# Mixer A's output projection: column blocks 2 and 3 as a pair with two seven-product units

## The chip, the cores and the metric

The kernel runs on one core of one Trainium2 chip. A core has five engines with a queue of instructions each: TensorE (matmuls; PE, with its weight loads shown as PEld), VectorE (DVE), ScalarE (ACT), GpSimd (POOL) and SyncE (SP, which here issues the weight loads). An engine starts its instructions in the order of its queue; semaphores make one engine wait for another. The metric is the device time of one launch in microseconds (us).

## The reference

The computation is an encoder of two layers on 256 tokens of width 2048, in float32. Layer 0 uses mixer A, layer 1 mixer B, and each is followed by a gated feed-forward block:

```python
for i in range(DEPTH):                       # DEPTH = 2
    hn = rms_norm(h, mix_norm[i])
    h = h + (mixer_a(hn, ...) if i % 2 == 0 else mixer_b(hn, ...))
    h = h + conv_ffn(rms_norm(h, ffn_norm[i]), w_up[i], conv_w[i], conv_b[i], w_down[i])
return rms_norm(h, final_norm)
```

Mixer A is attention with 16 query heads of width 128 and 4 key/value heads, with normalised and rotated queries and keys. Its last step is `o @ w_o`, with `o` of 256 x 2048 and `w_o` of 2048 x 2048. Mixer B ends in the same kind of product with a 3072 x 2048 matrix. The feed-forward block is `(silu(gate) * value) @ w_down` behind a product with `w_up` (2048 x 11264) and a width-3 convolution.

## The kernel before

**A product.** A float32 operand is split into a high part, rounded to the type `fp32r`, and a low part, the rest. A product is made of three matmuls: high x high, high x low, low x high (`feed`, lines 127 to 129). For weights the high part `wh` is written by ACT (L139) and the low part `wl` by DVE (L140). Both have four buffers (`NHL`), as has the raw tile `raw` that SP loads (`NRAW`). One `raw` holds 128 partitions x 1024 columns, two rows of 512.

**Chunks and column blocks.** The 2048 rows of a weight matrix go in chunks of 512 (`kg`, 0 to 3 in mixer A), its columns in blocks of 512 (`n`, 0 to 3). One `feed` multiplies one chunk with one block: two raw tiles, four slices of 128 rows, two halves of the tokens (`m`) and three matmuls, which makes 24 matmuls of 512 columns.

**Mixer A's output projection** is `out_proj`, called without `units`. `project2` does blocks 0 and 1, interleaved by chunk (cut at chunk 2, and chunk 3 last, since its heads leave the attention last). Then `project` does block 2 and, after it, block 3, chunk after chunk. After each block `add_residual` adds the two accumulators to `h` (DVE, L454), `post` takes sums of squares (ACT, L360) and starts `late_transpose`, which turns the block of `h` into the operand `xh` of the feed-forward block: two transposes on DVE (L370), 16 copies shared by POOL and ACT (L391, L389), then four high halves on ACT (L324) and four low halves on DVE (L327). The attention's outputs stand in tiles `a`, split by ACT and DVE (L320, L321).

**Units.** Mixer B's output projection and the feed-forward blocks' down projections have two column blocks done side by side by `pair`, in which a chunk may be a unit: `fast_unit` multiplies it with both blocks in seven products of recombined quarters in place of eight, 7 x 6 = 42 matmuls in place of 48. For that DVE makes four sums of weights (L173) beside seven splits (ACT L174, DVE L175). The products q = 1, 5, 6, 7 stand in the four banks of the pool `ps`, the others add to the accumulators of the two blocks, and `fold` (L187 to L204) brings the four into `h` with eight DVE additions of 512 columns. In mixer B the left operands are recombined by `recombined` (L797 to L817): four additions, eight subtractions on DVE for two chunks, and one split for each chunk.

**What sets the order.** Side work is written as generators. `step()` advances the first in the list `pending`, `step(True)` all in `beside`; each `feed` calls each twice, `fast_unit` four times the one and three times the other. Behind that a scheduler places the instructions of each engine by its own estimate of when they can run; `tc.high_priority` puts splits of weights ahead. What results is a fixed queue on each engine. The feed-forward block begins (`project2` with `late` = 1) with chunks 0, 1 and 2 of its first gate block, then the same of its first value block; chunk k needs block k of the turned `h`.

Of the kernel before, what the change touches and what calls it, by code (L numbers as in the profile page):

```python
# [7 lines left out]
F32 = mybir.dt.float32  # L8
F32R = mybir.dt.float32r
# [4 lines left out]
P = 128  # L14
D = 2048
NT = 256
# [14 lines left out]
def tile_encoder(ctx: ExitStack, tc: tile.TileContext, x, xT, w_a, w_ao, q_gain, k_gain, w_b, w_bo,  # L31
# [25 lines left out]
    def nm(s):  # L57
        uid[0] += 1
        return f"{s}_{uid[0]}"
# [16 lines left out]
        if next(gen, StopIteration) is not StopIteration:  # L76
            pending.append(gen)

    def step(mid=False):
        if mid:  # L80
            beside[:] = [g for g in beside if next(g, StopIteration) is not StopIteration]
            return
        while pending:
            if next(pending[0], StopIteration) is not StopIteration:
                return
            pending.pop(0)
        if spare and next(spare[0], StopIteration) is StopIteration:
            spare.pop(0)

    def drain(keep=0):  # L90
        while len(pending) > keep or beside:
            step(True)
            if len(pending) > keep:
                step()

    extra, count = [None], [0]

    def raw_tile():
        count[0] += 1
        if extra[0] and count[0] % 3 == 0:  # L100
            pool, tags = extra[0]
            tags.append(tags.pop(0))
            return pool.tile([P, 2, 512], F32, tag=tags[0], name=nm("raw"), bufs=2 if len(tags) == 1 else 1)
        return spool.tile([P, 2, 512], F32, tag="raw", name=nm("raw"), bufs=NRAW)

    def of_m(x, m):
# [99 lines left out]
    def pair(wd, ns, lhs, order, spot, folds, post, hurry=0, ready=None):  # L206
# [19 lines left out]
        for i, (kg, side) in enumerate(order):  # L226
            while ready is not None and kg not in ready:
                step()
            if side is None:
                if kg == fasts[0]:  # L230
                    while beside:
                        step(True)
                    while ready is not None and "u" not in ready:
                        step()
                    acc.update({q: ps_tile() for q in (1, 5, 6, 7)})
                later = {s for _, s in order[i + 1:]}
                end = [q for q, s in ((1, None), (5, None), (6, None), (7, None), (2, 0), (4, 0), (3, 1))
                       if not later & {None, s}]
                fast_unit(acc, lhs[-1 - kg], wd[ns[0], kg], wd[ns[1], kg], begun, end, spot)
                if kg == fasts[-1]:  # L240
                    beside.append(closing())
                    if 0 not in later:
                        finish(0)
                continue
            mine = ((2, 4), (3, 8))[side]
            end = not any(s in (side, None) for _, s in order[i + 1:])
            feed(sides[side], lhs, kg, wd[ns[side], kg], not begun.issuperset(mine), end,
                 begun=[m for m in range(2) if mine[m] in begun])
            begun.update(mine)
            for _ in range(hurry):  # L250
                if pending:
                    step()
            if end:
                finish(side)
# [230 lines left out]
    def ffn(l, hT, ss_in, cw, g_next, last, side=None):  # L485
        with tc.tile_pool(name=nm("fpool"), bufs=1) as fp:
# [156 lines left out]
            for hf, (p0, p1) in enumerate(HALVES):  # L643
                slots = {}
# [99 lines left out]

                np_ = p1 - p0
                wd = w_down[l][:, p0:p1]
                extra[0] = fp, ["raw2"]
# [21 lines left out]
    def out_proj(w, slots, kgs, late, g_next, junk, pool, tag, new_quad, cuts=(), units=None):  # L769
# [8 lines left out]
            post(n)  # L778

        if units:  # L780
            fast, own, tmp, spot, folds, raws = units
            done(project2(w, 0, 1, slots, kgs, late, lambda a: done(a, 0), None, cuts,
                          [lambda kg=kg: recombined(kg, slots, own, tmp) for kg in fast]), 1)
            extra[0] = raws
            both = {kg: [(kg, 0), (kg, 1)] for kg in sorted(kgs) if kg not in fast}
            (k0, k1, k2, k3), (f0, f1) = both, fast
            pair(w, (2, 3), slots, both[k0] + both[k1] + [(f0, None)] + both[k2] + [(f1, None)] + both[k3],
                 spot, folds, post)
            extra[0] = None
            drain(1)  # L790
            return hTn, ss
# [58 lines left out]
    def mixer_a():  # L850
        with tc.tile_pool(name="apool", bufs=1) as ap:
# [274 lines left out]
    def mixer_b(hT, ss_in):  # L1126
        with tc.tile_pool(name="bpool", bufs=1) as bp:
# [31 lines left out]
            for hf in range(2):  # L1159
# [160 lines left out]
                for g in range(3):  # L1320
                    accs = project(w_b, 6 * g + 4 + hf, hT, kgs)
                    vs[g] = evac_split(bp, accs, rstd, v12[g - 1] if g else None)
                    if g == 0:
                        start(value_stage())

            def own(kg):
                return pair_tile(bp, [P, 4, NT], "qT" if kg else "kT")

# [10 lines left out]
            return *out_proj(w_bo, slots, [0, 2, 4, 1, 3, 5], 3, 3, junk, bp, "vl", lambda: quad_tile(bp, "stg", 2),  # L1339
                             (), ((0, 2), own, tmp, spot, folds, (bp, ["e0", "e1"]))), cw  # L1340

    hT, ss, cw = mixer_a()
    hT, ss = ffn(0, hT, ss, cw, 2, False, bias_lines)
# [86 lines left out]
```

## Time and profile before

| | us |
|---|---|
| median of 3 runs (2240.21 to 2241.39) | 2241.18 |
| the profiled execution | 2241.6 |
| its span, first to last instruction | 2239.8 |
| mean granted TensorE clock | 0.999 |
| mixer A's block 2 and 3 of the output projection, in the span | about 215.7 to 259.3 |

Times within the span count from its first instruction. In a row of the timeline the first number is the start, the second the duration, and at its end may stand the idle time of the engine just before and what ended it; `x2` at the end merges two instructions that follow each other. A matmul's duration includes what overlaps with the next one, so the distance of two starts is the measure of its cost; the same holds, for a smaller part, on DVE. A row of a tile gives minimum, median and maximum duration in ns, then first and last start. A row of waits gives total us, number and the longest.

### The profile page before, as it was taken

What the parts mean: (1) busy time and instruction counts of PE and PEld (TensorE: products, weight loads), DVE (VectorE), ACT (ScalarE), POOL (GpSimd) and SP (SyncE); (2) the same over time, 40 slices, a digit from 0 to 9 for tenths busy, and PEclk for the clock granted to TensorE, in tenths of its full rate; (3) what the DMA queues carried; (4) which work ended last, traced back from release to release, by engine and by line L of the source; (5) the groups of instructions that cost most, each with busy time, mean ns of one, the idle gap of its engine ahead of it and who ended that gap; (6) DMA issues with size and microseconds to landing.
All of it is one profiled execution on the core that took longest, in us unless ns stands there. A gap on an engine that the chain in (4) does not pass through costs nothing.

```text
span 2239.8 us, 28736 instructions
## 1 busy us (share of the span) xinstructions
PE 2225.2 (99%) x10005; PEld 1843.6 (82%) x10005; DVE 1719.6 (77%) x2211; ACT 1320.1 (59%) x1858; POOL 784.2 (35%) x1035
## 2 busy tenths in 40 slices
PE   9999999999999999999999999999999999999998
PEld 7888888888888888888888888888888888888887
DVE  6877667778876778868876878587777798677795
ACT  7666655666545666755454456566655655455663
POOL 2343255652006563120053006003766500256601
PEclk9999999999999999999999999999999999999999
DMA  8565656555665565665556555556556566555653
GB/s 301 193 217 180 219 187 198 194 192 184 202 213 192 191 194 181 205 199 195 190 187 196 179 189 175 200 185 213 194 184 203 187 207 204 191 196 187 218 198 132
DMA packets 126178, 439.58 MB, mean 196 GB/s; under 512 B 14408, under 2 KB 18248, under 8 KB 126032
## 3 DMA queue, kind: packets, MB, share of 16 engines
q1 hardware_dynamic: 123056, 429.05, 57.2%
q0 software_dynamic: 2688, 8.39, 1.5%
q8 instruction: 78, 1.28, 0.2%
q14 instruction: 68, 0.56, 0.1%
q10 hardware_dynamic: 288, 0.30, 0.0%
HBM read 432.34 MB, written 5.34 MB: 195 GB/s over the span
## 4 chain that ended last, share of the span: by engine, by line
PE 90%; DVE 6%; issue 1%; ACT 1%; POOL 1%; DMA 1%; SPq 0%; DVEq 0%; POOLq 0%; ACTq 0%
PE acc L129 28%; PE acc L128 28%; PE acc L127 28%; DVE wl L175 2%; DVE wl L140 1%; DVE u L173 1%; PE ps L181 1%; PE ps L182 1%; PE ps L180 1%; DMA raw<-in_w_a_dram 1%; PE acc L181 1%; PE acc L182 1%; PE acc L180 1%; DVE cv L542 1%; ACT wh L139 0%
## 5 line engine op out<-in xcount | busy, mean ns | idle before, releaser
L140 DVE TENSOR_TENSOR wl<-raw,wh 128x1024 fp32r<-128x1024 f32 (+1 forms) x748 | 937.4, 1260 | 365.5 <-ACT wh L139 359.2
L139 ACT ACTIVATE wh<-raw 128x1024 fp32r<-128x1024 f32 (+1 forms) x748 | 782.6, 1049 | 643.8 <-PE acc L129 572.5
L127 PE MATMUL acc<-wh,xh 128*128 128x512 f32 x2176 | 849.2, 391 | 0.7 <-ACT wh L139 0.7
L128 PE MATMUL acc<-wl,xh 128*128 128x512 f32 x2176 | 848.2, 390 | 1.3 <-DVE wl L140 1.2
L129 PE MATMUL acc<-wh,xh 128*128 128x512 f32 x2176 | 847.3, 389 | 0.0
L555 POOL COPY u<-quad 32x256 f32<-32x256 f32 x672 | 483.7, 720 | 334.8 <-DVE quad L370 308.5
L128 PEld LDWEIGHTS acc<-wl,xh 128*128 128x128 f32 x2176 | 409.1, 188 | 87.3 <-DVE wl L140 3.8
L127 PEld LDWEIGHTS acc<-wh,xh 128*128 128x128 f32 x2176 | 409.0, 188 | 85.0 <-ACT wh L139 1.4
L129 PEld LDWEIGHTS acc<-wh,xh 128*128 128x128 f32 x2176 | 408.8, 188 | 84.4
L127 PE MATMUL acc<-wh,a 128*128 128x512 f32 x720 | 280.9, 390 | 0.0
L128 PE MATMUL acc<-wl,a 128*128 128x512 f32 x720 | 280.3, 389 | 0.0
L129 PE MATMUL acc<-wh,a 128*128 128x512 f32 x720 | 280.0, 389 | 0.0
L129 PEld LDWEIGHTS acc<-wh,a 128*128 128x128 f32 x720 | 135.1, 188 | 28.3 <-DVE a L321 0.2
L128 PEld LDWEIGHTS acc<-wl,a 128*128 128x128 f32 x720 | 135.2, 188 | 27.7
L127 PEld LDWEIGHTS acc<-wh,a 128*128 128x128 f32 x720 | 135.2, 188 | 27.5
L374 POOL COPY wide<-quad 32x256 f32<-32x256 f32 x133 | 89.1, 670 | 169.3 <-DVE quad L370 159.8
L391 POOL COPY wide<-quad 32x256 f32<-32x256 f32 x88 | 53.3, 605 | 223.4 <-DVE quad L370 155.7
L482 ACT ACTIVATE stg<-acc,rstd 128x512 f32<-128x512 f32 x122 | 82.9, 686 | 33.9 <-PE acc L129 33.9
L572 POOL TENSOR_TENSOR cv<-cg,cv 128x1024 f32<-128x1024 f32 x18 | 58.2, 3232 | 105.5 <-DVE cv L542 100.1
L174 ACT ACTIVATE wh<-raw 128x1024 fp32r<-128x1024 f32 x56 | 59.5, 1062 | 53.7 <-PE acc L129 48.9
L542 DVE SCALAR_TENSOR_TENSOR cg<-u,cw,cg 128x256 f32<-128x256 f32 x176 | 82.3, 511 | 4.5 <-ACT cg L534 4.5
L525 POOL MEMSET u<- 128x4 f32 x12 | 1.0, 106 | 231.3 <-DVE wl L175 211.0
(284 smaller groups left out, 2006.7 us busy)
## 6 DMA issues: line engine op xcount, KB each, us to landing
raw<-in_w_up_dram SPq DMA_DIRECT2D x352, 512.0 KB, 4.6
raw<-in_w_down_dram SPq DMA_DIRECT2D x176, 512.0 KB, 4.5
raw<-in_w_b_dram SPq DMA_DIRECT2D x144, 512.0 KB, 4.3
raw<-in_w_bo_dram SPq DMA_DIRECT2D x48, 512.0 KB, 4.2
raw<-in_w_a_dram SPq DMA_DIRECT2D x40, 512.0 KB, 4.7
raw<-in_w_ao_dram SPq DMA_DIRECT2D x32, 512.0 KB, 4.5
raw<-in_w_a_dram SPq DMA_DIRECT2D x16, 256.0 KB, 5.9
there<-quad POOLq DMA_DIRECT2D x6, 512.0 KB, 3.5
```

What stands on the lines that cost most here:

```text
L127: nc.tensor.matmul(accs[m], xh, wh[:, j, :], start=st, stop=False)
L128: nc.tensor.matmul(accs[m], xh, wl[:, j, :], start=False, stop=False)
L129: nc.tensor.matmul(accs[m], xl, wh[:, j, :], start=False, stop=sp)
L139: nc.scalar.activation(wh[:, c], r[:, c], AF.Copy)
L140: nc.vector.tensor_tensor(wl[:, c], r[:, c], wh[:, c].bitcast(F32), ALU.subtract)
L174: nc.scalar.activation(wh, r, AF.Copy)
L374: nc.gpsimd.tensor_copy(o[32 * c:32 * c + 32, :, 32 * q:32 * q + 32], quad[32 * q:32 * q + 32, c])
L391: nc.gpsimd.tensor_copy(dst, src)
L482: nc.scalar.activation(o[:, m, :], accs[m], AF.Copy, scale=rstd[:, m:m + 1])
L542: nc.vector.scalar_tensor_tensor(cj, halves(flat[:, j, o:o + NT])[:, ::-1], tap(n, j, i), cj, ALU.mult, ALU.add)
L555: nc.gpsimd.tensor_copy(o, src)
L572: made.append(eng.tensor_tensor(cv, cg, cv, ALU.mult).ins)
```

## The change

In mixer A, blocks 2 and 3 now go through `pair`, in the order chunk 2 (block 2, block 3), chunk 0 as a unit, chunk 3 (block 2), chunk 1 as a unit, chunk 3 (block 3). `recombined` for chunks 0 and 1 starts at the end of `project2`. The order of chunks is now given by the caller; mixer B's stays as it was. The recombination's four tiles (`tmp`), and every third raw tile during the pair, take their space from the four buffers of a tag `pT`, which holds the turned probabilities of the attention: high and low part now stand in one tile of `[P, 2, 4, P]` where they had a tile each. `pair` steps the side work until a unit's operands are there, and `step` and `drain` take a number of generators to leave unstarted (`keep`).

```diff
-    def step(mid=False):
+    def step(mid=False, keep=0):
...
             pending.pop(0)
+            if pending and len(pending) <= keep:
+                return
...
             if len(pending) > keep:
-                step()
+                step(keep=keep)
...
-            return pool.tile([P, 2, 512], F32, tag=tags[0], name=nm("raw"), bufs=2 if len(tags) == 1 else 1)
+            return pool.tile([P, 2, 512], F32, tag=tags[0][0], name=nm("raw"), bufs=tags[0][1])
...
             if side is None:
+                while -1 - kg not in lhs:
+                    step()
...
         if units:
-            fast, own, tmp, spot, folds, raws = units
+            fast, order, own, tmp, spot, folds, raws = units
...
-            both = {kg: [(kg, 0), (kg, 1)] for kg in sorted(kgs) if kg not in fast}
-            (k0, k1, k2, k3), (f0, f1) = both, fast
-            pair(w, (2, 3), slots, both[k0] + both[k1] + [(f0, None)] + both[k2] + [(f1, None)] + both[k3],
-                 spot, folds, post)
+            pair(w, (2, 3), slots, order, spot, folds, post)
...
-            rp = ap.tile([P, 2, 2, P], F32, tag="pTh", name="rp", bufs=4)
-            gbs = ap.tile([P, 4, P], F32, tag="pTl", name="gbs", bufs=4)
+            rp = ap.tile([P, 2, 2, P], F32, tag="pT", name="rp", bufs=4)
+            gbs = ap.tile([P, 4, P], F32, tag="pT", name="gbs", bufs=4)
...
             def new_pT():
-                return pair_tile(ap, [P, 4, P], "pT", 4)
+                t = ap.tile([P, 2, 4, P], F32R, tag="pT", name=nm("pT"), bufs=4)
+                return t[:, 0], t[:, 1]
...
+            def own(kg):
+                return pair_tile(ap, [P, 4, NT], "qT" if kg else "kT")
+
+            def tmp():
+                return ap.tile([P, 4, NT], F32, tag="pT", name=nm("tmp"), bufs=4)
+
+            def spot(i):
+                return ap.tile([P, 2, 512], F32, tag=("vh", "vl", "ro")[i], name=nm("sum"))
+
+            def folds():
+                return [ap.tile([P, 2, 512], F32, tag=t, name=nm("fold")) for t in ("stg", "ro")]
+
+            order = [(2, 0), (2, 1), (0, None), (3, 0), (1, None), (3, 1)]
             return *out_proj(w_ao, slots, kgs, 1, 1, junk, ap, "t2",
-                             lambda: pair_slot(16, [P, 4, 8, 32], name="quad"), (2,)), cw
+                             lambda: pair_slot(16, [P, 4, 8, 32], name="quad"), (2,),
+                             ((0, 1), order, own, tmp, spot, folds, (ap, [("pT", 4)]))), cw
```

More of the change, by code (lines that the diff above doesn't have):

```diff
@@ L746, in ffn @@
                 wd = w_down[l][:, p0:p1]
-                extra[0] = fp, ["raw2"]
+                extra[0] = fp, [("raw2", 2)]
                 if last and hf == 1:
@@ L1324, in mixer_b @@
                         start(value_stage())
+            both = {kg: [(kg, 0), (kg, 1)] for kg in (1, 3, 4, 5)}
+            order = both[1] + both[3] + [(0, None)] + both[4] + [(2, None)] + both[5]
             def own(kg):
@@ L1339, in mixer_b @@
             return *out_proj(w_bo, slots, [0, 2, 4, 1, 3, 5], 3, 3, junk, bp, "vl", lambda: quad_tile(bp, "stg", 2),
-                             (), ((0, 2), own, tmp, spot, folds, (bp, ["e0", "e1"]))), cw
+                             (), ((0, 2), order, own, tmp, spot, folds, (bp, [("e0", 1), ("e1", 1)]))), cw
     hT, ss, cw = mixer_a()
```

## The prediction

> **What bounds the kernel now.** I read the totals first, then who waits for whom, then windows, then the order of instructions in time. The totals, and one row of the chain that ended last:
>
> ```profile
> span 2239.8 us, 28736 instructions
> PE 2225.2 (99%) x10005; PEld 1843.6 (82%) x10005; DVE 1719.6 (77%) x2211; ACT 1320.1 (59%) x1858; POOL 784.2 (35%) x1035
> PE 90%; DVE 6%; issue 1%; ACT 1%; POOL 1%; DMA 1%; SPq 0%; DVEq 0%; POOLq 0%; ACTq 0%
> ```
>
> TensorE (PE) is busy for 99% of the span: a matmul that goes is worth its full pitch, a wait costs its full length. All waits of PE:
>
> ```profile
> PE ps L336 <- DVE qTl L321: 2.0, 1, 2.0
> PE ps L181 <- DVE wl L175: 1.6, 4, 0.4
> PE acc L128 <- DVE wl L140: 1.2, 3, 0.6
> PE acc L127 <- ACT wh L139: 0.7, 1, 0.7
> ```
>
> There are few, and all but one are for VectorE (DVE): it is next in line. Four windows (us; busy PE, PEld, DVE, ACT, POOL; granted clock; DMA): mixer A's output projection, the units of mixer B's, the units in a feed-forward block, and a stretch at half clock.
>
> ```profile
> 205.00:259.00 54.00, 54.00 (x239) 44.59 (x239) 36.77 (x46) 39.13 (x69) 13.06 (x24) 1.00 0.58 192
> ...
> 1478.00:1519.00 41.00, 41.00 (x183) 33.95 (x182) 36.35 (x37) 25.69 (x29) 1.13 (x1) 1.00 0.53 181
> 535.00:560.00 25.00, 24.63 (x107) 19.73 (x106) 23.25 (x26) 14.30 (x17) 0.00 (x0) 1.00 0.54 182
> ...
> 145.00:148.40 3.40, 3.40 (x11) 2.82 (x11) 2.12 (x4) 1.08 (x4) 0.00 (x0) 0.51 0.90 278
> ```
>
> Where the change is made, DVE works 36.77 of 54 us and PE never waits. Where units run, DVE works 36.35 of 41 and 23.25 of 25.
>
> **The change part by part.** *Matmuls.* A chunk of two column blocks costs 2 x 24 matmuls plain and 7 x 6 = 42 as a unit, so two units save 12. TensorE's order in time:
>
> ```profile
> 204.82 0.40 PE L127 MATMUL acc<-wh,a 128*128 128x512 f32 x1
> ...
> 207.11 0.62 PE L129 MATMUL acc<-wh,a 128*128 128x512 f32 x2
> ...
> 259.28 0.39 PE L127 MATMUL acc<-wh,xh 128*128 128x512 f32 x1
> ...
> 270.16 0.39 PE L127 MATMUL acc<-wh,xh 128*128 128x512 f32 x1
> ...
> 303.70 0.39 PE L128 MATMUL acc<-wl,xh 128*128 128x512 f32 x1
> ```
>
> From 270.16 to 303.70 lie 148 steps of 0.2266 us, all on the path: 12 x 0.2266 = **-2.7 us**. This is all that the change can win, and 0.12% of the span; about 0.2% (4.5 us) is what a measurement of this kernel can tell from no change.
>
> *DVE's new work.* It is costed by start-to-start times. Mixer B's fold and feed-forward entry, then the recombination's tiles:
>
> ```profile
> 1508.58 2.35 DVE L140 TENSOR_TENSOR wl<-raw,wh 128x1024 fp32r<-128x1024 f32 x2
> 1510.85 0.68 DVE L195 TENSOR_TENSOR fold<-ps,fold 128x512 f32<-128x512 f32 x1
> 1511.45 0.68 DVE L197 TENSOR_TENSOR fold<-ps,fold 128x512 f32<-128x512 f32 x1
> ...
> 1516.41 1.30 DVE L370 STREAM_TRANSPOSE quad<-h 128x512 f32<-128x512 f32 x2
> 1517.64 1.18 DVE L140 TENSOR_TENSOR wl<-raw,wh 128x1024 fp32r<-128x1024 f32 x1
> ```
> ```profile
> 268.29 1.66 DVE L327 SCALAR_TENSOR_TENSOR xh<-wide,gain,xh 128x256 fp32r<-128x256 f32 x4
> ```
> ```profile
> L802 DVE TENSOR_TENSOR tmp<-a x4: 679/723/879, 1384.6 to 1393.0; 128x512 f32<-128x512 f32 x4
> L809 DVE TENSOR_TENSOR tmp<-tmp x4: 409/420/610, 1388.3 to 1430.7; 128x256 f32<-128x256 f32 x4
> L809 DVE TENSOR_TENSOR tmp<-tmp,tmp x4: 418/464/611, 1391.1 to 1432.6; 128x256 f32<-128x256 f32 x4
> ```
>
> So a split or sum of 1024 columns takes 2.27/2 = 1.14, a 512-column add 0.60, a quad transpose 0.62, a low half of xh 0.41. Neighbours overlap by some 0.08, so a recombining add takes 0.64, a subtraction 0.34 or 0.38. A unit has 7 splits and 4 sums: 11 x 1.14 = 12.5 us of DVE under 42 x 0.2266 = 9.5 us of PE. Mixer B lays two plain feeds (10.9 us of PE, four splits, 4.6 of DVE) between its units; here there is one (5.4 against 2.3).
>
> *First wait: the last attention outputs.* In the changed kernel's DVE order most of the recombination of both chunks (4 adds, 4 subtractions) stands ahead of the last split `a` of the attention, which chunk 3 needs. DVE there, before:
>
> ```profile
> 200.77 1.22 DVE L140 TENSOR_TENSOR wl<-raw,wh 128x1024 fp32r<-128x1024 f32 x1
> 201.91 0.42 DVE L321 TENSOR_TENSOR a<-ps,a 128x256 fp32r<-128x256 f32 x1
> 202.24 1.73 DVE L140 TENSOR_TENSOR wl<-raw,wh 128x1024 fp32r<-128x1024 f32 x1
> 203.89 0.74 DVE L321 TENSOR_TENSOR a<-ps,a 128x256 fp32r<-128x256 f32 x2
> 205.40 1.23 DVE L140 TENSOR_TENSOR wl<-raw,wh 128x1024 fp32r<-128x1024 f32 x1 [0.76 <-ACT wh L139]
> 206.54 0.42 DVE L321 TENSOR_TENSOR a<-ps,a 128x256 fp32r<-128x256 f32 x1
> ```
>
> Inserted are 4 x 0.64 + 2 x 0.34 + 2 x 0.38 = 4.0 us, less the 0.76 idle at 205.40: 3.2. The split ends at 206.96 + 3.2 = 210.2. PE wants it at 207.11, and with two matmuls of the other block now ahead (0.45) at 207.6: a wait of **2.6** (1.5 to 3.5). Behind it on PE stand all later matmuls, behind the split on DVE all later weight splits.
>
> *Second wait: feed-forward entry.* DVE's queue from 210.2 to the split of the second weight piece of feed-forward chunk 0: 4 subtractions 1.5; 24 splits 27.4; 8 sums 9.1; splits of the two recombined operands 2.3; 8 residual adds 4.8; 8 fold adds 4.8; 6 quad transposes 3.7; 8 low halves 3.3. Sum **56.9**, ending at 267.1 without one idle moment. The last 11 of these (two residual adds of block 3, six adds of the fold, two transposes of block 2, the split: 7.2 us) cannot start before the projection's last matmuls have ended, and the split that PE wants 3.2 us into the feed-forward block stands behind them all.
>
> DVE will also idle, above all at the low halves of block 1, which follow eight POOL copies begun by a transpose shortly before:
>
> ```profile
> 1517.87 6.04 POOL L391 COPY wide<-quad 32x256 f32<-32x256 f32 x8 [53.42 <-ACT wh L139]
> ```
>
> The copies take 6.0 and ACT's half 0.5, while DVE has about 5.2 to do in between (three splits, three adds): some 1.3 us; starts that wait for matmuls add a little. I take 1.7 (0.5 to 3.5), hence 268.8. PE started that piece 14 matmuls after 259.28, at 262.45: late by **6.3**, which contains the first wait and the 2.7 saved.
>
> *One-hot matmuls.* The changed order runs the four bias-table matmuls inside this wait; here they stand, on PE's path:
>
> ```profile
> 368.24 0.47 PE ps L1121 x2
> 379.62 0.47 PE ps L1121 x2
> ```
>
> Their 4 x 0.2266 = 0.9 us go there: **-0.9**.
>
> *Block 2's turn.* Chunk 2 of the feed-forward block needs the turned block 2, formerly made under block 3. Walked the same way (transpose, 6.0 us of copies, halves, transposes of block 3), its second weight split is late by **0.8** (0 to 2); mixer B's entry has a wait of this kind, within PE's 1.2 above.
>
> *Clock.* Half clock follows one wait of the trace:
>
> ```profile
> 142.45 0.28 PE L335 MATMUL ps<-kTl,qTh 128*128 128x256 f32 x1
> 144.68 0.41 PE L336 MATMUL ps<-kTh,qTl 128*128 128x256 f32 x1 [1.95 <-DVE qTl L321]
> ...
> 145.54 0.63 PE L127 MATMUL acc<-wh,xh 128*128 128x512 f32 x1
> ...
> 148.10 0.51 PE L127 MATMUL acc<-wh,xh 128*128 128x512 f32 x1
> ```
>
> Six steps take 2.56 us there, 0.427 each: 3.4 us at 0.51 lose 3.4 x (1 - 0.2266/0.427) = 1.6. The entry wait (6.3 + 2.7 - 2.6 - 0.9, less about 1 us lost inside the units: some 4.5) is over twice 1.95, so I count it once, less what block 2's lateness hides: **+1.0** (0 to 3, if the first wait does it too).
>
> The Trainium skill ("TensorE: Matmul & The Clock Gate", Part 1) has the half clock come only after an idle window of about 3.4 us. The row above differs: a wait of 1.95 us sufficed. By the page the first wait would be free of it and the clock term 0 to 1.0 (a sum of 6.0 to 7.0 us), by the row up to 1.6 more.
>
> *At nothing.* Shared pT tiles hold the same bytes in the same number, and the order on DVE, ACT and PE up to the recombination is unchanged; a slip there is 0 to 1 us. Weight loads on SP now also wait for the recombination's tiles; they stand a unit (9.5 us) ahead of their use, and a load lands sooner:
>
> ```profile
> raw<-in_w_ao_dram SPq DMA_DIRECT2D x32, 512.0 KB, 4.5
> ```
>
> The `keep` edit moves halves and transposes at mixer B's entry, where a wait of about 0.5 may go or grow: **-0.2** (-0.5 to +0.5).
>
> Sum: 6.3 - 0.9 + 0.8 + 1.0 - 0.2 = **+7.0 us**. The profiled execution took 2241.6 (span 2239.8), 0.4 above the median of 2241.18; on the median, **2248.2**.
>
> **Rivals.** *DVE keeps up* (not slower): the splits stay ahead by wh/wl's four buffers, and only the 12 matmuls show: 2241.2 - 2.7 = 2238.5. For it: mixer B's units ran with PE 41.00 of 41. Against: the tighter spacing and the fold behind the last matmul. It decides if DVE's queue ends below 262.45 - 2.7 = 259.7, that is if 56.9 us shrink by 7.
>
> *The delay is half hidden*: DVE never idles (4.6 late), the clock stays full, block 2 is in time: 4.6 - 0.9 - 0.5 = +3.2, 2244.4.
>
> *Loads become the wait*: loads of w_down stand ahead of w_up's in SP's queue at the feed-forward entry and wait for block 2's halves; if they hold up two w_up loads by 2 us each, and both waits halve the clock, +7.0 + 4 + 1.6: 2253.8.
>
> **How the numbers follow.** Forecast (between +4.5 and +11.3) 0.70; half hidden (-1 to +4.5) 0.17; keeps up 0.09; loads 0.04. The forecast's own range by its bounds is 2245.7 to 2252.5. Half of the half-hidden case brings the low end to 2243.0, which leaves about 0.2 outside. Slower by over 0.2%: 0.70 + 0.04 and a little for median scatter, 0.75; faster needs more than the 2.7 saved, 0.02; within, 0.23.
>
> **What would show it.** 12 fewer matmuls; a wait of PE near 207 for DVE's `a`; one of 4 to 5 us near 264 for `wl`; a clock below 1.00 after it; DVE busy for over 90% from 205 to 270. Wrong if these waits stay under 1 us each, or if PE waits for loads.

## The result and the profile after

| | before | after |
|---|---|---|
| median, us | 2240.49 (6 runs) | 2252.93 (6 runs, 2251.47 to 2256.04) |
| the profiled execution | 2241.6 | 2252.98 |
| its span | 2239.8 | 2251.2 |
| mean granted clock | 0.999 | 0.996 |

The change makes the kernel slower, by a ratio of 1.0058 with a 95% interval of 1.0047 to 1.0068, 12.4 us by the medians. The forecast was 2248.2, with 2252.5 as the upper end of its range: the direction was right, the size too small.

The totals of the profile after:

```profile
span 2251.2 us, 28764 instructions
PE 2226.7 (99%) x9993; PEld 1843.9 (82%) x9993; DVE 1747.3 (78%) x2247; ACT 1328.8 (59%) x1867; POOL 791.3 (35%) x1035
```

The 12 matmuls are gone (x10005 became x9993), and the span is 11.4 us longer. So TensorE loses about 14 us to waits and to a lower clock. Its waits, after, beside two that were there before, 1.5 us at the start of the kernel and 1.9 in the attention (total us, number, longest; lines from 100 on are a few higher than before, L142 and L177 are the splits `wl`, L325 the split `a`):

```profile
PE acc L130 <- DVE wl L142: 5.7, 2, 5.5
PE acc L131 <- DVE a L325: 2.5, 2, 1.7
PE ps L183 <- DVE wl L177: 2.3, 5, 0.8
PE ps L182 <- ACT wh L176: 1.7, 1, 1.7
PE acc L129 <- ACT wh L141: 1.0, 1, 1.0
```

The timeline shows where the new ones stand (start, duration, and idle time of PE before):

```profile
203.82 0.40 PE L130 MATMUL acc<-wl,a 128*128 128x512 f32 x1
205.07 0.50 PE L131 MATMUL acc<-wh,a 128*128 128x512 f32 x1 [0.85 <-DVE a L325]
...
207.26 0.39 PE L130 MATMUL acc<-wl,a 128*128 128x512 f32 x1
209.33 0.73 PE L131 MATMUL acc<-wh,a 128*128 128x512 f32 x2 [1.68 <-DVE a L325]
...
232.36 0.39 PE L184 MATMUL acc<-wh,kTl 128*128 128x512 f32 x1
234.47 0.50 PE L182 MATMUL ps<-wh,kTh 128*128 128x512 f32 x1 [1.72 <-ACT wh L176]
235.72 0.50 PE L183 MATMUL ps<-wl,kTh 128*128 128x512 f32 x1 [0.76 <-DVE wl L177]
...
236.75 0.56 PE L184 MATMUL ps<-wh,kTl 128*128 128x512 f32 x1
...
240.63 0.39 PE L182 MATMUL ps<-wh,kTh 128*128 128x512 f32 x1
...
267.00 0.40 PE L1138 MATMUL ps<-oh,rl 128*24 128x512 f32 x1
272.88 0.80 PE L130 MATMUL acc<-wl,xh 128*128 128x512 f32 x1 [5.48 <-DVE wl L142]
...
278.23 0.39 PE L129 MATMUL acc<-wh,xh 128*128 128x512 f32 x1
```

By distances of starts, less one pitch of 0.2266: the first wait has two pieces, 1.02 and 1.84 us (2.9); the first unit waits 1.88 and 1.03 (2.9); the feed-forward entry waits 5.65. Behind two of these places the clock halves. The windows below (busy time of PE, PEld, DVE, ACT, POOL; then the granted clock) are laid on the borders at which the clock changes, 3.413 us apart:

```profile
206.11:209.52 3.41, 1.73 (x8) 1.13 (x7) 3.38 (x6) 0.00 (x0) 0.00 (x0) 1.00 0.74 265
209.52:212.94 3.42, 3.42 (x16) 2.81 (x16) 2.93 (x7) 2.06 (x3) 0.00 (x0) 1.00 0.64 182
...
233.42:236.83 3.41, 1.61 (x6) 1.12 (x7) 2.38 (x3) 3.41 (x5) 0.00 (x0) 1.00 0.01 5
236.83:240.24 3.41, 3.41 (x10) 2.67 (x9) 3.41 (x4) 1.82 (x3) 0.00 (x0) 0.50 0.00 0
...
267.55:270.96 3.41, 0.00 (x0) 0.00 (x0) 3.41 (x6) 2.23 (x7) 0.00 (x0) 1.00 0.00 0
270.96:274.37 3.41, 1.50 (x4) 1.21 (x5) 3.41 (x5) 3.21 (x9) 2.46 (x2) 0.50 0.10 29
274.37:277.79 3.42, 3.42 (x10) 2.65 (x9) 1.12 (x1) 0.77 (x2) 3.17 (x7) 0.50 0.91 303
```

Three windows at half clock are new. The starts give their price: from 236.75 to 240.63 ten steps take 3.88 us where 2.27 is usual, a loss of 1.6; from 272.88 to 278.23 thirteen steps take 5.35 where 2.95 is usual, a loss of 2.4. The first of the last two windows costs little, since TensorE still waits in most of it.

So: 2.9 + 2.9 + 5.65 + 1.6 + 2.4 - 2.7 (matmuls) = 12.7. The four one-hot matmuls stand in no term: both kernels run them, here ahead of the entry wait, at 266.31 to 267.00. Measured directly, the matmul that starts at 195.00 before starts at 193.78 after, and the first one of the feed-forward block's down projection starts at 521.40 before and at 533.26 after. So the stretch between them became 13.1 us longer; waits too short for the list make the rest. Ahead of it the kernel after is 1.2 us earlier (0.81 of this is a wait at 136.4 in the attention, which comes and goes with the experiments' kernels), and 0.45 us of a wait at 1527.3, in the feed-forward block behind mixer B, is gone: 13.1 - 1.2 - 0.45 gives the 11.4 between the spans.

DVE, over the stretch for which the prediction asked for more than 90%:

```profile
205.00:270.00 65.00, 58.17 (x244) 46.32 (x244) 59.92 (x74) 44.13 (x66) 15.24 (x16) 0.97 0.45 154
```

59.92 of 65 us is 92%.

### The profile page after: what moved, and what is told of

It reads as the page before. It is cut to its first block, busy times and chain, and to the rows that moved or that the text cites. A ratio compares the mean times of both kernels' runs of the same rounds, so it can differ in the third digit from the quotient of the medians.

```text
span 2251.2 us, 28764 instructions
## 1 busy us (share of the span) xinstructions
PE 2226.7 (99%) x9993; PEld 1843.9 (82%) x9993; DVE 1747.3 (78%) x2247; ACT 1328.8 (59%) x1867; POOL 791.3 (35%) x1035
## 3 DMA queue, kind: packets, MB, share of 16 engines
q8 instruction: 78, 1.28, 0.2%
## 4 chain that ended last, share of the span: by engine, by line
PE 83%; DVE 5%; issue 1%; ACT 1%; POOL 0%; POOLq 0%; DVEq 0%; ACTq 0%
PE acc L130 26%; PE acc L131 26%; PE acc L129 26%; DVE wl L177 2%; PE ps L183 1%; PE ps L184 1%; DVE u L175 1%; PE ps L182 1%; PE acc L183 1%; PE acc L184 1%; PE acc L182 1%; DVE wl L142 0%; DVE cv L546 0%; PE ps L1290 0%; PE ps L336 0%
## 5 line engine op out<-in xcount | busy, mean ns | idle before, releaser
L142 DVE TENSOR_TENSOR wl<-raw,wh 128x1024 fp32r<-128x1024 f32 (+1 forms) x740 | 926.5, 1259 | 344.9 <-ACT wh L141 339.0
L141 ACT ACTIVATE wh<-raw 128x1024 fp32r<-128x1024 f32 (+1 forms) x740 | 773.8, 1049 | 632.8 <-PE acc L131 555.5
L131 PE MATMUL acc<-wh,a 128*128 128x512 f32 x688 | 267.6, 389 | 2.5 <-DVE a L325 2.5
L129 PE MATMUL acc<-wh,a 128*128 128x512 f32 x688 | 268.4, 390 | 0.0
L130 PE MATMUL acc<-wl,a 128*128 128x512 f32 x688 | 267.9, 389 | 0.0
L131 PEld LDWEIGHTS acc<-wh,a 128*128 128x128 f32 x688 | 129.1, 188 | 30.2 <-DVE a L325 3.4
L129 PEld LDWEIGHTS acc<-wh,a 128*128 128x128 f32 x688 | 129.2, 188 | 26.4
L130 PEld LDWEIGHTS acc<-wl,a 128*128 128x128 f32 x688 | 129.2, 188 | 26.4 <-DVE wl L142 0.2
L395 POOL COPY wide<-quad 32x256 f32<-32x256 f32 x88 | 62.1, 706 | 249.2 <-DVE quad L374 187.8
L378 POOL COPY wide<-quad 32x256 f32<-32x256 f32 x133 | 88.1, 663 | 168.3 <-DVE quad L374 159.8
L176 ACT ACTIVATE wh<-raw 128x1024 fp32r<-128x1024 f32 x64 | 68.0, 1062 | 56.2 <-PE acc L131 48.8
L177 DVE TENSOR_TENSOR wl<-raw,wh 128x1024 fp32r<-128x1024 f32 x64 | 77.9, 1223 | 2.8 <-ACT wh L176 2.3
```

The costliest lines, as they stand in the source:

```text
L129: nc.tensor.matmul(accs[m], xh, wh[:, j, :], start=st, stop=False)
L130: nc.tensor.matmul(accs[m], xh, wl[:, j, :], start=False, stop=False)
L131: nc.tensor.matmul(accs[m], xl, wh[:, j, :], start=False, stop=sp)
L141: nc.scalar.activation(wh[:, c], r[:, c], AF.Copy)
L142: nc.vector.tensor_tensor(wl[:, c], r[:, c], wh[:, c].bitcast(F32), ALU.subtract)
L176: nc.scalar.activation(wh, r, AF.Copy)
```

## The experiments

All ratios are to the kernel before, measured on the same chip as the kernel in question; their intervals are 0.0009 to 0.0013 to either side (2 to 3 us), so differences of less than that between two experiments are not taken for settled by the ratios. The last table of this part puts them side by side.

**Are the units the cause, or the tiles and the `keep` edit?**

```diff
-                             lambda: pair_slot(16, [P, 4, 8, 32], name="quad"), (2,),
-                             ((0, 1), order, own, tmp, spot, folds, (ap, [("pT", 4)]))), cw
+                             lambda: pair_slot(16, [P, 4, 8, 32], name="quad"), (2,)), cw
```

> The changed kernel without the two units: blocks 2 and 3 of mixer A's output projection go one after the other again (plain feeds), while the shared pT tiles and the keep edit stay. Theory (VectorE's queue around the units makes all of the loss): the time of the kernel before, 2240.5 us, give or take 0.5 (the keep edit alone: PE's wait of 0.4 to 0.5 us at mixer B's entry may go); no wait of PE near 207, 233 or 267 us. Rival (the shared pT tiles or the keep edit cost something of their own): 2242 us or more, with a new wait in the attention or at mixer B's entry.

Measured: 0.9994 (0.9986 to 1.0003). From 195 to 330 us PE has no wait at all. Shared tiles and `keep` cost nothing that can be measured; the units carry the whole loss.

**Is it the sum of VectorE's work?** First its largest part is left out, then also the recombination. In `fast_unit`, for mixer A alone (`bare`):

```diff
-        t1, t2, t4 = (spot(i) for i in range(3))
+        t1, t2, t4 = (b22, b12, b21) if bare else (spot(i) for i in range(3))
...
-                if q in sums:
+                if q in sums and not bare:
                     nc.vector.tensor_tensor(*sums[q], ALU.add)
...
```

> The changed kernel with the eight sums of weights left out in mixer A's two units (the three splits of each unit that take a sum take a raw tile instead, so the output projection is not the reference's); all else stays. It takes 8 x 1.14 = 9.1 us from VectorE alone; TensorE, ScalarE and the loads do the same as before. Theory (VectorE's sum of work decides the entry): the entry wait (6.0 us with what follows) falls under 1 us, both half-clock stretches go (4.8 us lost), the first wait (2.9) stays since it lies ahead of the units: ratio 0.9995 to 1.001. Rival (the chain through the last matmul, fold, transposes and GpSimd decides, or the loads): an entry wait of over 3 us and a half clock behind it stay, ratio 1.003 or more.

Measured: 1.0017 (1.0008 to 1.0027). PE's waits between 195 and 330 us, all of them:

```profile
PE acc L131 <- DVE a L325: 2.7, 2, 1.7
PE acc L130 <- DVE wl L142: 1.3, 2, 1.0
PE acc L183 <- DVE wl L177: 0.3, 1, 0.3
```

The entry wait is 1.0 in place of 5.5, the unit's waits are gone, no half clock is left in that stretch, and the first wait stays, as the theory said; 1.0017 is a little above its range. Taking 9.1 us of DVE's work gave back 9.2 us (1.0058 - 1.0017 of 2240); that the two agree so closely is chance, since each ratio is known to 2 or 3 us. The fold stands in the same place as in the changed kernel, so the chain behind the last matmul alone does not make the long entry wait. One thing else changed with the sums: GpSimd's copies of block 0 took 4.48 us in place of 9.76, those of block 1 took 9.92 in place of 6.07 (see below). Then:

```diff
+    def plain_quarters(kg, slots):
+        (hi0, lo0), (hi1, lo1) = ([slots["t", kt][:, o::2, :] for o in range(2)] for kt in (4 * kg, 4 * kg + 2))
+        left, right = (hi0[:, :, :P], lo0[:, :, :P]), (hi1[:, :, P:], lo1[:, :, P:])
+        slots[-1 - kg] = {q: left if q in (1, 5, 6, 3) else right for q in range(1, 8)}
+        yield
...
-                          [lambda kg=kg: recombined(kg, slots, own, tmp) for kg in fast]), 1)
+                          [lambda kg=kg: plain_quarters(kg, slots) if late == 1 else recombined(kg, slots, own, tmp) for kg in fast]), 1)
```

> The changed kernel with mixer A's eight sums of weights and its whole recombination left out (the units multiply raw tiles and plain quarters of the attention's output, so the output projection is not the reference's); units, order, fold and loads stay. It asks whether the units are worth their 12 matmuls once VectorE's extra work is gone: 9.1 us of sums, 5.5 of recombination and 2.3 of splits less than in the changed kernel. Theory: no first wait, no wait in the units, an entry wait of at most 1 us (the fold is still behind the last matmul), no half clock after it: 2.7 us saved less 0 to 1: ratio 0.9988 to 0.9995. Rival (the pair has a cost beside VectorE's sums and recombination, such as the fold's chain): ratio 1.0005 or more.

Measured: 1.0004 (0.9995 to 1.0013), between the two expectations and nearer to the rival's. The first wait is gone. But the 2.7 us do not show even now; PE's waits from 195 to 330 us are

```profile
PE ps L183 <- DVE wl L177: 0.8, 1, 0.8
PE acc L130 <- DVE wl L142: 0.6, 2, 0.4
PE ps L182 <- ACT wh L176: 0.3, 1, 0.3
```

With the sums and the recombination the pair loses 12 to 13 us; with neither it about breaks even. Why the last 2 to 3 us do not show, beyond these short waits, stays open.

**Where the first wait comes from, and what it is worth.** The recombination's twelve operations go to GpSimd (`eng` is `nc.gpsimd` in mixer A):

```diff
-            nc.vector.tensor_tensor(r[:, 2 * b:2 * b + 2], hi.bitcast(F32), lo.bitcast(F32), ALU.add)
+            eng.tensor_tensor(r[:, 2 * b:2 * b + 2], hi.bitcast(F32), lo.bitcast(F32), ALU.add)
...
-            nc.vector.tensor_tensor(s[:, o], x, y, ALU.subtract)
+            eng.tensor_tensor(s[:, o], x, y, ALU.subtract)
```

> The changed kernel with mixer A's four additions and eight subtractions of the recombination on GpSimd instead of VectorE. Theory (the recombination ahead of the last split a makes the first wait): the gaps at 203.8 and 207.3 us (2.9 us together) shrink under 0.5; VectorE has 5.5 us less to do, 1.5 of it behind the first wait, so the entry wait near 267 us (6.0 with what follows) falls by about 1.5 at most; in all 3 to 4.5 us less, about 2249. GpSimd may be late with the subtractions; then a wait stands at the first unit near 232 us. Rival (the first wait comes from the pT tiles that the recombination and the extra raw tiles share, or from a load): the first wait stays, 2252.9.

Measured: 1.0069 (1.0055 to 1.0082). The first wait fell from 2.5 to 0.8 in the waits (under 0.5 was expected), so the recombination on DVE makes most of it. But the time did not fall, against the expected 2249. A row of DVE and the last of the recombination on POOL:

```profile
226.77 1.23 DVE L175 TENSOR_TENSOR sum<-raw,raw 128x1024 f32<-128x1024 f32 x1 [6.48 <-DMA raw<-in_w_ao_dram]
```
```profile
216.24 2.54 POOL L810 TENSOR_TENSOR tmp<-tmp,tmp 128x256 f32<-128x256 f32 x2
```

GpSimd needs until 218.8 for the recombination. An extra raw tile lies in the space of `tmp`; DVE stood idle for 6.48 us for its load. Without the extra raw tiles:

```diff
-                             ((0, 1), order, own, tmp, spot, folds, (ap, [("pT", 4)]), nc.gpsimd)), cw
+                             ((0, 1), order, own, tmp, spot, folds, None, nc.gpsimd)), cw
```

> The recombination on GpSimd as before, and the extra raw tiles taken out as well. With the recombination on GpSimd alone VectorE idled 6.5 us for a weight load into a tile of the space that the late recombination still used. Theory (that load is why 5.5 us less of VectorE work won nothing): the idle of 6.5 us goes, the first wait stays at about 1 us, the first unit waits under 1.5 us, the entry wait is 2 to 4 us: ratio 1.002 to 1.004. Rival (GpSimd's recombination is too slow in itself, some 21 us from 202 to 223 us, and the first unit waits for its operands, or copies behind it come late): over 3 us of waits near the first unit stay, ratio 1.0055 or more.

Measured: 1.0052 (1.0039 to 1.0066); the idle of 6.48 us is gone, the entry wait is 3.3. The ratio lies between the two expectations; the rival's sign came true, waits of 3.7 us stand in the units. The other way to take the first wait away starts the recombination behind the loop over blocks 0 and 1:

```diff
-            done(project2(w, 0, 1, slots, kgs, late, lambda a: done(a, 0), None, cuts,
-                          [lambda kg=kg: recombined(kg, slots, own, tmp) for kg in fast]), 1)
+            behind = [lambda kg=kg: recombined(kg, slots, own, tmp) for kg in fast]
+            if late == 1:
+                accs = project2(w, 0, 1, slots, kgs, late, lambda a: done(a, 0), None, cuts)
+                for gen in behind:
+                    start(gen())
+                done(accs, 1)
...
```

> The changed kernel with the recombination of both chunks started behind the attention's end instead of at the end of the loop over blocks 0 and 1; of its eight operations ahead of the attention's last split, four remain (two additions, two subtractions, 2.0 us in place of 4.0). Theory (VectorE's sum of work decides, waits only move): the first wait falls from 2.9 to about 1.2 us, and what is gained comes back as a wait in the units or at the entry, since VectorE does the same work until then: ratio 1.005 to 1.006, as the changed kernel. Rival (waits add up one by one): 1.5 to 2 us are gained, ratio 1.0045 to 1.005, with the entry wait as long as before.

Measured: 1.0047 (1.0034 to 1.0059). The first wait is 1.3, the entry waits 4.0 and 1.0 in two places, with one stretch of half clock in place of two. The ratio lies on the edge between the two expectations and does not tell them apart. The profile does, in part: the stretch from 195 to 521 us is 9.9 us longer than before, where it was 13.1, so 3.2 us were gained, more than the rival expected. The waits did not only move: the first unit's went too, and gaps of 1.3 and 0.9 us came up in the second.

**Do the extra raw tiles matter, taken alone?**

```diff
-                             ((0, 1), order, own, tmp, spot, folds, (ap, [("pT", 4)]))), cw
+                             ((0, 1), order, own, tmp, spot, folds, None)), cw
```

> The changed kernel without the extra raw tiles: during the pair every weight load goes into the four usual raw buffers, none into the space of the turned probabilities. Theory (VectorE's queue makes the waits, loads do not): no wait of PE goes, the ratio to the kernel before stays at 1.005 to 1.0065; if anything loads now come later, in the first unit. Rival (the loads into shared tiles, queued behind the recombination that uses them, make the wait near 232 us): the gaps at 232 to 235 us (2.9 together) and the half clock at 236 us (1.6 lost) go, ratio 1.0035 to 1.004.

Measured: 1.0062 (1.0048 to 1.0075). The rival's gaps did go (2.9 became 0.5), and the half clock behind them. Yet the time is the same: at 248 to 251 us stand two new gaps of 0.8, and the entry wait grew from 5.5 to 6.4. Here a wait taken away ahead of a full DVE queue came back further down. So loads are not what bounds this stage. That the gaps went does not by itself make loads their cause: in this kernel block 0's copies also took 5.27 us only, since they ran ahead of DVE's sums (see below), and the run does not separate the two:

```profile
219.16 5.27 POOL L395 COPY wide<-quad 32x256 f32<-32x256 f32 x8 [17.55 <-DVE quad L374]
```

**Is the fold behind the last matmul to blame?**

```diff
-            order = [(2, 0), (2, 1), (0, None), (3, 0), (1, None), (3, 1)]
+            order = [(2, 0), (0, None), (2, 1), (1, None), (3, 0), (3, 1)]
```

> The changed kernel with the pair's order chunk 2 (block 2), unit 0, chunk 2 (block 3), unit 1, chunk 3 (block 2), chunk 3 (block 3): two plain feeds behind the last unit, as mixer B has them, so that the fold of the units need not stand behind the last matmul. Theory A (VectorE's queue is full from 209 to 272 us, so its sum decides): what VectorE does is the same, the entry wait loses at most 1 to 2 us, and waits in the units, which now have one feed less ahead of them, grow by as much: 2251 to 2255 in all. Theory B (the fold behind the last matmul makes the entry wait): the six fold additions and two residual additions, 4.8 us, leave the stretch behind the end, the entry wait falls from 6.0 to under 2 us and the half clock after it goes (3.2 us lost): about 2246.

Measured: 1.0046 (1.0034 to 1.0059), between A and B and nearer to A. Both effects showed: the entry wait fell to 2.1 us with one stretch of half clock, and the units, which had less work ahead of them, have six gaps of 0.4 to 0.8 us, 3.3 by distances of starts. The fold's place is a part of the entry wait, worth less than the 7 us that B promised.

**GpSimd's copies.** In the changed kernel the eight copies of block 0's turn took 9.76 us, where the prediction assumed 6.0. ScalarE's high halves waited for them, and the split `wh` of the unit's first sum stood behind those. POOL's, ACT's and DVE's rows of after:

```profile
221.97 9.76 POOL L395 COPY wide<-quad 32x256 f32<-32x256 f32 x8 [20.23 <-DVE quad L374]
...
231.76 1.71 ACT L328 ACTIVATE xh<-wide,gain 128x256 fp32r<-128x256 f32 x4 [3.27 <-POOL wide L395]
233.37 1.04 ACT L176 ACTIVATE wh<-sum 128x1024 fp32r<-128x1024 f32 x1
...
232.30 0.49 DVE L331 SCALAR_TENSOR_TENSOR xh<-wide,gain,xh 128x256 fp32r<-128x256 f32 x1 [1.28 <-ACT xh L328]
234.44 1.23 DVE L177 TENSOR_TENSOR wl<-sum,wh 128x1024 fp32r<-128x1024 f32 x1 [1.65 <-ACT wh L176]
```

Block 0's copies all on ScalarE:

```diff
-            if i % 2:
+            if i % 2 or act:
...
-            start(late_transpose(hTn, n, g_next, pool, tag, new_quad))
+            start(late_transpose(hTn, n, g_next, pool, tag, new_quad, tag == "t2" and n == 0))
```

> The changed kernel with all 16 copies of block 0's turn on ScalarE (8 of them were on GpSimd, where they took 9.76 us beside VectorE's run of sums and splits). Theory (GpSimd's slow copies hold up ScalarE's high halves and with them the split wh of the first unit's sum, queued behind): PE's gaps at 232.4 and 234.5 us (2.9 together) and the half clock at 236.6 us (1.6 lost) go, and VectorE's 1024-column splits and sums at 223 to 231 us come back from about 1.34 us apart to 1.14; VectorE loses 2.9 us of idle time, so the entry wait grows no more than PE's start of it moves ahead: 2248 to 2250 in all. Rival (the first unit is late because four sums and seven splits are too much for VectorE in one place, whatever GpSimd does): gaps of 2 us or more stay near 232 us, 2252 to 2254.

Measured: 1.0053 (1.004 to 1.0065), above the theory's range, in the rival's, and not clear of the changed kernel's interval. The gaps at the unit fell from 2.9 to 0.9 and the half clock behind them went, so the rival's sign is absent; but a new gap of 1.2 us stands at 256 and the entry wait is as long as ever. From the last split `a` to the split that ends the entry wait DVE needs 61.6 us in place of 63.5, and the stretch from 195 to 521 us is 11.6 us longer than before in place of 13.1: some 1.5 us were gained, where 3 to 5 were expected. DVE idles anew, 0.54 and 1.30 us, for splits `wh` of ScalarE, which now has all the copies. DVE's sums beside the copies came back to their pace, as expected; first a group of after from 222.9 to 231.1, then the same of this kernel from 216 to 233 (last columns: busy us, mean ns, idle):

```profile
L175 DVE TENSOR_TENSOR sum<-sum,raw 128x1024 f32<-128x1024 f32 x2 | 2.8, 1412 | 0.0
```
```profile
L175 DVE TENSOR_TENSOR sum<-sum,raw 128x1024 f32<-128x1024 f32 x2 | 2.4, 1218 | 0.0
```

**One unit.** With half of DVE's extra work, a wait that goes should stay gone. Three steps, each on top of the one before:

```diff
-            order = [(2, 0), (2, 1), (0, None), (3, 0), (1, None), (3, 1)]
+            order = [(1, 0), (1, 1), (2, 0), (0, None), (2, 1), (3, 0), (3, 1)]
...
-                             ((0, 1), order, own, tmp, spot, folds, (ap, [("pT", 4)]))), cw
+                             ((0,), order, own, tmp, spot, folds, (ap, [("pT", 4)]))), cw
```

> The changed kernel with one unit instead of two: chunk 1 plain in both blocks, chunk 2 (block 2), unit 0, then three plain feeds. TensorE saves 6 matmuls (1.36 us). Theory (VectorE's queue): of the 19.4 us that two units add to VectorE (recombination 5.5, splits of the recombined operands 2.3, fold 4.8, sums 9.1, less two splits 2.3) 12.2 remain, against 17 us that it idles in the kernel before between 205 and 259 us; the first wait falls from 2.9 to about 0.7, the entry wait from 6.0 to under 1.5, no half clock follows: ratio 0.9995 to 1.001. Rival (the entry wait is the chain through the fold, the transposes and GpSimd's copies, which one unit has as well): entry wait over 3 us with a half clock, ratio 1.003 or more.

Measured: 1.0021 (1.0012 to 1.0031), between the two. No wait over 0.9 us at the entry and no half clock, but a first wait of 1.8 and waits of 2.1 in the unit. In this order three feeds stand behind the unit, so the run doesn't separate the fold's place from DVE's smaller sum of work.

The second step starts the recombination late, by the edit shown above:

> The kernel with one unit, its recombination also started behind the attention's end (one addition and two subtractions fewer ahead of the last split). With one unit VectorE has room, so here a wait that goes should stay gone: the first wait of 2.2 us falls under 1, ratio 1.001 to 1.002 (1.0021 with the early recombination). If it comes back elsewhere, 1.002 or more.

Measured: 1.0028 (1.0017 to 1.0039): the first wait fell to 0.9, but it came back elsewhere, as 2.8 and 0.5 in the unit. GpSimd's copies stand ahead of it again:

```profile
224.80 10.66 POOL L395 COPY wide<-quad 32x256 f32<-32x256 f32 x8 [4.91 <-DVE xh L331]
```
```profile
235.50 1.70 ACT L328 ACTIVATE xh<-wide,gain 128x256 fp32r<-128x256 f32 x4 [4.71 <-POOL wide L395]
237.11 1.04 ACT L176 ACTIVATE wh<-raw 128x1024 fp32r<-128x1024 f32 x1
```

ACT stood 4.71 us at the head of a queue in which the unit's next split came right behind, and two stretches of half clock followed (237.5 to 244.3). The third step takes the copies of blocks 0 and 1 from GpSimd (`n < 2` in the edit for block 0):

> The kernel with one unit and late recombination, and all copies of the turns of blocks 0 and 1 on ScalarE instead of half of them on GpSimd. With one unit the waits in the unit (2.8 us) stood behind ScalarE's high halves, which waited for GpSimd's copies. If that is their cause, they fall under 1 us and the ratio to the kernel before is 0.9998 to 1.001, the 1.36 us of saved matmuls against what is left of the waits; if ScalarE (6.7 us of copies in each turn) becomes late itself, the waits stay and the ratio is 1.0015 or more.

Measured: 1.0016 (1.0007 to 1.0024). The two waits at the unit and the half clock are gone; a 0.9 us wait for another split and small ones at the feed behind it are left. The cause of those two waits is shown; the ratio of up to 1.001 that was expected from it was missed. It is the best of the kernels with a unit that compute the reference, and still slower than the kernel before. What a better one could win is small: 1.36 us for one unit, 2.7 for two.

Side by side, from 195 to 330 us: PE's listed waits and the time at half clock; then how much longer than before the stretch between the matmuls at 195.00 and 521.40 us (of the kernel before) became, in one profile of each kernel; and the ratio.

| kernel | first wait | in units and plain feeds | entry | half clock | stretch | ratio |
|---|---|---|---|---|---|---|
| after | 2.5 | 2.5 | 5.5 | 10.2 | 13.1 | 1.0058 |
| recombination on GpSimd | 0.8 | 4.9 | 3.8 | 10.2 | 14.6 | 1.0069 |
| the same, no extra raw | 0.8 | 3.7 | 3.3 | 6.8 | 11.2 | 1.0052 |
| late recombination | 1.3 | 1.8 | 5.0 | 3.4 | 9.9 | 1.0047 |
| no extra raw | 2.7 | 2.0 | 6.4 | 6.8 | 12.8 | 1.0062 |
| two feeds last | 2.7 | 2.2 | 2.5 | 3.4 | 10.1 | 1.0046 |
| block 0's copies on ScalarE | 2.7 | 1.7 | 5.5 | 6.8 | 11.6 | 1.0053 |
| no sums | 2.7 | 0.3 | 1.3 | 0 | 3.2 | 1.0017 |
| no sums, no recombination | 0 | 1.1 | 0.6 | 0 | 0.4 | 1.0004 |
| one unit | 1.8 | 2.1 | 0.7 | 0 | 5.6 | 1.0021 |
| one unit, late recombination | 0.9 | 3.3 | 0 | 6.8 | 6.4 | 1.0028 |
| the same, copies on ScalarE | 0.9 | 2.2 | 0 | 0 | 3.4 | 1.0016 |

The view lists no short waits, so a row's columns do not sum to its stretch. The stretch leaves out most of the attention, whose time differs by up to 3.6 us from profile to profile.

## Why the prediction was right in kind and too small

**Right.** Twelve matmuls fewer. The kernel's shared tiles and `keep` edit at about nothing (0.9994 without the units). DVE's queue as the cause: busy for 92% of the stretch, and every one of the 68 operations that the prediction counted between the last split `a` and the split that ends the entry wait is there, in that number. The first wait: 2.9 us by starts, predicted 2.6 (1.5 to 3.5), though in two pieces and not one. One-hot matmuls inside the entry wait. Loads no cause; the rival that put them down at 2253.8 came near the measured time by chance. The rival "DVE keeps up" needed 7 us less of DVE's work; with 9.1 less the entry wait was 1.0.

**The step that failed is the second wait, "late by 6.3", and in it DVE's idle time, "I take 1.7 (0.5 to 3.5), hence 268.8".** The split was ready at 272.8, and PE went on at 272.88, 10.4 us behind 262.45. In the prediction's own terms the sum is 10.4 (6.3 predicted) - 0.9 + 0 (0.8) + 2.4 (1.0) - 0.45 (-0.2) = 11.5, against 11.4 between the spans. What DVE did there that was not priced, besides the idle moments of 1.28 and 1.65 us shown above at 232.30 and 234.44:

```profile
208.86 0.42 DVE L325 TENSOR_TENSOR a<-ps,a 128x256 fp32r<-128x256 f32 x1
...
211.19 1.23 DVE L142 TENSOR_TENSOR wl<-raw,wh 128x1024 fp32r<-128x1024 f32 x1 [0.45 <-ACT wh L141]
...
263.42 1.68 DVE L331 SCALAR_TENSOR_TENSOR xh<-wide,gain,xh 128x256 fp32r<-128x256 f32 x4 [1.28 <-ACT xh L328]
...
271.64 3.85 DVE L142 TENSOR_TENSOR wl<-raw,wh 128x1024 fp32r<-128x1024 f32 x3
```

That is 4.7 us of idle time, and six splits and sums 1.34 us apart in place of 1.14 add 1.2. From 209.3, with 56.9 of work, 4.7, 1.2 and 0.7 of shorter gaps and rounding, the split ends at 272.8, and not at 268.8. The idle time at block 1's low halves (263.42) was priced rightly, "some 1.3 us". What the prediction left out is the same thing at block 0, in the middle of the first unit: there the copies priced at 6.0 us took 9.76, DVE idled 2.9 us behind them, and its operations beside them were slower by 1.2. Of these 4.1 us the kernel with block 0's copies on ScalarE had 1.9 back; it idled for ScalarE instead, so for the rest the origin is read from the rows and not shown by a run. The 6.0 came from mixer B, where DVE did shorter work beside the copies (last section). On PE it showed as "about 1 us lost inside the units", which was 2.9 and 1.6 more at half clock.

**The second mis-sized term is the clock, "I count it once ... +1.0 (0 to 3)".** Behind the entry it measured 2.4, within its bounds: the wait left one whole window without work and the next with 1.50 of 3.41 us, and each halved the one that follows. The half clock in the unit, which the prediction did not have, is no further term of its sum: it lies ahead of the entry, where DVE is the later one.

The bounds given for the terms add up to +3.7 and +12.7. The range drawn from them, +4.5 to +11.3, was narrower, and the measured time lies just above it.

**Too high.** Block 2's turn (+0.8): no wait of PE is listed there. The `keep` edit (-0.2): a wait of 0.45 us at mixer B's entry is not in the profile after.

**The rule weighed in the prediction** was the Trainium skill's, "TensorE: Matmul & The Clock Gate", Part 1. By it the first wait would be free of the half clock. The trace agrees there: no half clock follows 205 to 209 us. It does not agree that an idle window must precede: 1.61 us of work in the window before 236.83 did not keep the full clock.

**What stays open.** What a window at half clock costs the kernel was not measured alone, since here none comes without a wait. The starts give its price on PE, but where DVE is the bound it may cost less: without the extra raw tiles one went, and the stretch is shorter by only 0.3 us.

## What to carry to other kernels

When a change trades TensorE's work for VectorE's, walk VectorE's queue over the whole stage and not operation by operation. Waits along a full queue don't simply add up: an edit that removes one may show it, or a part of it, further down, so compare the whole stretch. Price GpSimd's copies by what VectorE does beside them, and look at which queue stands behind the instruction that waits for them. A long wait of TensorE is to be priced by the clock's windows: one window at half clock for each in which TensorE has worked less than about half, at the price of the work that falls into it.

## What the runs showed of the hardware

**The clock goes by windows of 3.413 us, and about half a window of idle is enough.** PE's busy time in a window, and the clock of the next: 1.73 of 3.41 us, full (after, 206.11); 1.61 and 1.50, half (after, 233.42 and 270.96). The limit lies near these figures, but it is not sharp in the profile's busy time, whose matmul ends are modelled: 1.68 kept the full clock (the kernel without sums, 141.61), and 1.86 did not in the kernel with the recombination on GpSimd and no extra raw tiles. Its window, and one of the kernel with the recombination on GpSimd:

```profile
248.03:251.44 3.41, 1.86 (x7) 0.80 (x6) 3.41 (x4) 3.35 (x4) 3.28 (x4) 1.00 0.63 202
251.44:254.86 3.42, 3.42 (x10) 2.65 (x9) 3.42 (x4) 2.14 (x5) 1.24 (x1) 0.50 0.60 199
```
```profile
265.31:268.72 3.41, 1.62 (x7) 0.99 (x6) 3.41 (x7) 2.79 (x3) 0.00 (x0) 1.00 0.06 10
268.72:272.13 3.41, 3.41 (x10) 2.37 (x9) 3.41 (x6) 1.48 (x3) 0.00 (x0) 0.50 0.42 144
```

The windows don't start with a wait: in the profile after, half clock begins at 144.67, 236.83 and 270.96, 27 and 10 windows apart. So the same wait can go either way. Before, a wait of 1.95 us at 142.5 halved the clock; the kernel without units has it too (a distance of starts of 2.11 us beyond the pitch, from 141.70 to 143.93), but there it falls across the border of two windows, neither of which is short of work by half, and the clock stays full (the borders are counted on from 6.65, where this kernel's clock first becomes full):

```profile
139.77:143.18 3.41, 2.21 (x11) 1.69 (x9) 3.41 (x5) 2.81 (x4) 2.57 (x1) 1.00 0.93 288
143.18:146.59 3.41, 2.66 (x14) 2.27 (x14) 3.18 (x6) 0.03 (x1) 0.00 (x0) 1.00 0.75 182
```

The Trainium skill ("TensorE: Matmul & The Clock Gate", Part 1) calls the window free-running, and these rows agree.

**GpSimd's copies and VectorE's long operations slow each other.** The copies of blocks 0 to 2, one by one (minimum, median, maximum in ns), before and after:

```profile
L391 POOL COPY wide<-quad x24: 392/397/1296, 213.7 to 245.0; 32x256 f32<-32x256 f32 x24
```
```profile
L395 POOL COPY wide<-quad x24: 391/1211/1304, 222.0 to 277.5; 32x256 f32<-32x256 f32 x24
```

The median copy went from 397 to 1211 ns. The stretch of mixer B's copies before, from which the prediction took its 6.0 us, and that of block 0's copies after (busy time of PE, PEld, DVE, ACT, POOL):

```profile
1517.87:1523.91 6.04, 6.04 (x29) 4.99 (x28) 5.52 (x7) 5.48 (x13) 5.75 (x8) 1.00 0.29 92
```
```profile
221.97:231.73 9.76, 9.76 (x45) 8.09 (x44) 9.05 (x7) 6.38 (x11) 9.46 (x8) 1.00 0.47 162
```

In both, seven DVE operations lie beside eight copies; what differs most is their length (in the second all have 1024 columns, in the first only two). So the copies went at about the pace of DVE's operations. In the second stretch a sum on DVE took 1412 ns; with the copies on ScalarE it took 1218. The Trainium skill ("SBUF — State Buffer", Who interferes with whom) says that a VectorE instruction with two SBUF inputs and a GpSimd instruction that reads SBUF exclude each other for the length of an instruction; one copy for each of VectorE's operations agrees with that.
